# The last feature tile in two token halves, with the closing norm and the writes per half

## The chip, the cores and the metric

The kernel is one program on one core of a Trainium2 chip. The time is the device time of one execution, in microseconds. Before the change three runs gave 2014.44, 2014.51 and 2013.72, so the median is 2014.44. The profile is one further execution.

## The reference

Two blocks run one after the other on 512 tokens of 1024 features, in float32. The first is a transformer-like block. The second has two layers, each with a gated linear recurrence and a matrix memory beside each other. Only the end of the second block matters here:

```python
        y = jnp.concatenate([y_rg, y_ml], axis=-1) @ w_out[l]
        x = x + gate[:, None, :] * y
    return rms_norm(x, final_g)
```

So the last layer ends with a product by `w_out` (2048 by 1024), a gated addition to the residual, and a norm over all 1024 features of each token, scaled by `final_g`.

## The kernel before, in words

Activations lie transposed: features on the 128 partitions, the 512 tokens along the free axis. A tensor of 1024 features is eight tiles of 128x512, here called feature tiles, numbered `m`. Every float32 matrix product is three matmuls in a reduced format: `mm3` (L121 to L127) multiplies the high part of the weights by the high part of the activations (L125), high by low (L126) and low by high (L127).

Weights come as a stream of 512 KB chunks. For each chunk SyncE issues a DMA (L81), ScalarE rounds it to the high part (L96) and VectorE subtracts to get the low part (L98). By the time the last tile starts, all chunks have been loaded and split.

At the end of layer 1 the loop over `m` makes each feature tile of the output product from 16 input tiles `d`, so 48 matmuls of 512 columns into one bank of PSUM. VectorE multiplies the bank by the layer's gate and adds the residual (L1880; the tile is called `xr`). ScalarE squares the result (L149), and VectorE and GpSimd add the squares up (L153, L155, L159). `early` sums the first seven tiles' squares over the partitions, with matmuls against a column of ones (L165), in the middle of the last tile's products.

After the last tile the closing norm begins. `mean` sums the last tile's squares over the partitions (L165) and adds the early part (L180, tile `nms`). `rsqrt` is ten small VectorE operations (L207 to L214), each of which waits for the one ahead of it, and ends in `ncol`, one value for each token. `part2` spreads these values over all partitions with four matmuls against the identity (L195), and ScalarE copies the result to SBUF (L199, `nrow`). Then VectorE multiplies the eight feature tiles by `final_g` and `nrow` (L2041) and SyncE issues one write of 256 KB for each (L2042).

The program has no planner. Each engine takes its instructions strictly in the order in which the code issues them, and waits are on semaphores that count instructions of other engines.

Of the kernel before, what the change touches and what calls it, by code (L numbers as in the profile page):

```python
# [21 lines left out]
F32 = mybir.dt.float32  # L22
# [3 lines left out]
AF = mybir.ActivationFunctionType  # L26
OP = mybir.AluOpType
# [4 lines left out]
T = 512  # L32
DM = 1024
# [87 lines left out]
def mm3(k, ps, w, x, start, stop):  # L121


    mm = k.nc.tensor.matmul
    mm(ps, w[0], x[0], start=start, stop=False)  # L125
    mm(ps, w[0], x[1], start=False, stop=False)  # L126
    mm(ps, w[1], x[0], start=False, stop=stop)  # L127


class Norm:  # L130
# [9 lines left out]
    def add(self, src, scale=1.0):  # L140


        k, i = self.k, self.i
        own = i < 2 or (self.tail and i == self.n - 1)
        if own:
            sq = self.pool.tile([128, T], F32, name="nacc", bufs=3 if self.pool is k.work else 6)
        else:
            sq = k.work.tile([128, T], F32, name="nsq", bufs=2)
        k.nc.scalar.activation(sq, src, AF.Square, scale=scale)  # L149
        if own:  # L150
            self.acc.append(sq)
        elif i % 2:
            k.nc.gpsimd.tensor_add(self.acc[1], self.acc[1], sq)  # L153
        else:
            k.nc.vector.tensor_add(self.acc[0], self.acc[0], sq)  # L155
        self.i += 1
        if self.i == self.n - self.tail:
            eng = k.nc.vector if self.tail else k.nc.gpsimd
            eng.tensor_add(self.acc[0], self.acc[0], self.acc[1])  # L159
# [14 lines left out]
    def mean(self, eps=1e-6):  # L174
        k, v = self.k, self.k.nc.vector
        assert self.i == self.n
        self.ms = k.work.tile([128, 4], F32, name="nms", bufs=2)
        s = self.colsums(self.acc[2 if self.tail else 0])
        if self.tail:
            v.scalar_tensor_tensor(self.ms, s, 1.0 / DM, self.head, op0=OP.mult, op1=OP.add)  # L180
        else:
            v.tensor_scalar(self.ms, s, 1.0 / DM, eps, op0=OP.mult, op1=OP.add)
# [19 lines left out]
def rsqrt(k, out, ms):  # L202

    nc = k.nc
    shape = list(ms.shape)
    seed = k.work.tile(shape, I32, name="rseed", bufs=2)
    nc.vector.tensor_scalar(seed, ms.bitcast(I32), -0.5, 1597463007.0, op0=OP.mult, op1=OP.add)  # L207
    y = seed.bitcast(F32)
    for it in range(3):
        a = k.work.tile(shape, F32, name="rsa", bufs=2)  # L210
        nc.vector.tensor_mul(a, y, y)
        nc.vector.scalar_tensor_tensor(a, a, -0.5, ms, op0=OP.mult, op1=OP.mult)
        y2 = out if it == 2 else k.work.tile(shape, F32, name="rsy", bufs=2)
        nc.vector.scalar_tensor_tensor(y2, a, 1.5, y, op0=OP.add, op1=OP.mult)  # L214
        y = y2
# [11 lines left out]
def xtile(k, name, dtype=F32R):  # L227
    return k.xp.tile([128, T], dtype, name=name, tag="x", bufs=26)
# [29 lines left out]
def bank(k):  # L258
    k.nbank = (k.nbank + 1) % 2
    tag = ("pa", "pb")[k.nbank]  # L260
    return k.ps.tile([128, T], F32, name=tag + k.phase, tag=tag, bufs=2)
# [1109 lines left out]
def between(k, scr, nf, ng):  # L1371

    nc, v = k.nc, k.nc.vector
    gg = k.work.tile([128, 8], F32, name="gg")
    gf = k.vec[:, VEC["norm_final"][0]:VEC["norm_final"][0] + 8]
    v.tensor_mul(gg, gf, k.lay[0].gs)
    nf.part1(root=False)
    ng.mean()  # L1380
    ms = k.work.tile([128, 4], F32, name="nmt", bufs=2)
    v.scalar_tensor_tensor(ms, nf.ms, 1e-6, ng.ms, op0=OP.mult, op1=OP.add)
    ng.col = k.work.tile([128, 4], F32, name="ncol", bufs=2)
    rsqrt(k, ng.col, ms)
    k.tail[1]()
    ng.part2()
    k.tail[2]()
    xs = modulate(k, 0, ng, gg, scr)
    k.tail[3]()
    rsqrt(k, nf.col, nf.ms)  # L1390

    def root():
        nf.part2()

    def residual(d):
        v.scalar_tensor_tensor(k.h[d], k.h[d], gf[:, d:d + 1], nf.row, op0=OP.mult, op1=OP.mult)
        nc.sync.dma_start(scr["x"][d], k.h[d])
        k.dbg(f"x2{d}", k.h[d])
    return xs, [root] + [lambda d=d: residual(d) for d in range(8)]


def renorm(k, l, norm, scr):
    norm.part1()
    norm.part2()
    xs = modulate(k, l, norm, k.lay[l].gs, scr)
    return xs, [lambda d=d: k.nc.sync.dma_start(scr["x"][d], k.h[d]) for d in range(8)]
# [2 lines left out]
LAYER = """P24 U24 P25 U25 P20 qkv0 D P21 U20 U21 mi2 vw P22 U22 P23 U23 qkv1 D mi3 vw P0 U0 qkv2 vw D qkv3 g0 vw g1 P1 U1 ri0 P8 g2 D P9 U8 g3 hw0 hs0 U9 rg0 rq0 vr0 P26 U26 hn0 rs0 rs1 rz0 rz1 vr1 P27 U27 hw1 f0 P2 U2 hs1 D P3 U3 ri1 u F0 P32 U32 P33 U33 D rg1 rq1 hn1 rs2 P10 U10 P11 f1 rs3 U11 P29 U29 rz2 hw2 P28 rz3 vr2 U28 P4 U4 hs2 P5 U5 ri2 u P34 rg2 rq2 F1 U34 P35 U35 hn2 rs4 P12 D P13 f2 D U13 U12 rs5 P31 rz4 vr3 hw3 P30 rz5 U30 U31 P6 U6 P7 U7 ri3 D u hs3 D P36 F2 rg3 U36 P37 rq3 hn3 rs6 P14 U37 rs7 u P15 f3 U14 U15 rz6 P38 D F3 rz7 U38 D P39 U39 vw"""  # L1409


def layer(k, l, xs, aside, ins, scr, norm):


    nc, v = k.nc, k.nc.vector
    L = k.lay[l]
    with ExitStack() as st:
        pool = st.enter_context(k.tc.tile_pool(name=f"lay{l}", bufs=1))
# [323 lines left out]
        cat = {}  # L1742
# [120 lines left out]
        xr = {}  # L1863

        def x_read(m):
            if m < 8:
                xr[m] = xtile(k, "xr", F32)
                nc.sync.dma_start(xr[m], scr["x"][m])
        k.phase = f"out{l}"
        for m in range(8):  # L1870
            x_read(m)
        for m in range(8):
            ps = bank(k)
            for d in range(16):
                k.ws.hold = m == 7 and d >= 8
                if m == 7 and d == 10:
                    norm.early()
                mm3(k, ps, k.ws.get((f"w_out.{l}", d, m)), cat[d], d == 0, d == 15)
            k.h[m] = xr[m]
            v.scalar_tensor_tensor(k.h[m], ps, L.mod[:, 16 + m:17 + m], k.h[m], op0=OP.mult, op1=OP.add)  # L1880
            norm.add(k.h[m])
# [21 lines left out]
def body(tc, ins, out, dbg):  # L1903
    nc = tc.nc
    with ExitStack() as ctx:
        k = Ctx()
        k.nc, k.tc = nc, tc
        ctx.enter_context(tc.manual_schedule())
        pool = lambda name, bufs=1, **kw: ctx.enter_context(tc.tile_pool(name=name, bufs=bufs, **kw))
# [9 lines left out]
        scr = {"wq": dp.tile([2, 128, 128], F32, name="scr_wq"), "V": dp.tile([8, 128, 512], F32, name="scr_V"),  # L1919
               "C": dp.tile([8, 128, 512], F32, name="scr_C"), "T": dp.tile([8, 128, 512], F32, name="scr_T"),  # L1920
               "R": dp.tile([8, 2, 128, 256], F32, name="scr_R"), "u": dp.tile([512, 512], F32, name="scr_u"),
               "y": dp.tile([512, 512], F32, name="scr_y"), "x": dp.tile([8, 128, T], F32, name="scr_x"),
               "v": dp.tile([4, 2, 128, T], F32, name="scr_v")}
# [11 lines left out]
        for d in range(8):  # L1935
            t = xtile(k, "h", F32)
# [29 lines left out]
        norm = Norm(k, 8)  # L1966
        xs = []
# [31 lines left out]
        with tc.tile_pool(name="prep2", bufs=1) as pp:  # L1999
# [6 lines left out]
            with ple_p as lp:  # L2006
# [15 lines left out]
                with tc.tile_pool(name="sums", bufs=1) as np_:  # L2022
# [6 lines left out]
                    xs, aside = between(k, scr, nf, ng)  # L2029
        norm = None  # L2030
        for l in range(2):
            norm = Norm(k, 8, tail=True)
            k.phase = f"layer{l}"
            layer(k, l, xs, aside, ins, scr, norm)
            if l == 0:
                xs, aside = renorm(k, 1, norm, scr)
        norm.part1()
        norm.part2()
        for d in range(8):
            o = xtile(k, "out", F32)  # L2040
            nc.vector.scalar_tensor_tensor(o, k.h[d], k.v("final_g_2", d), norm.row, op0=OP.mult, op1=OP.mult)  # L2041
            nc.sync.dma_start(out[d * 128:(d + 1) * 128], o)  # L2042
        return k.ws


# [108 lines left out]
def build(dbg=None):  # L2154
    import concourse.bacc as _bacc
    import concourse.tile as _tile
    from concourse import mybir as _mybir
    nc = _bacc.Bacc("TRN2", target_bir_lowering=False, num_devices=1)
    ins = {n: nc.dram_tensor(f"in_{n}_dram", s, F32, kind="ExternalInput").ap() for n, s in SHAPES.items()}
    out = nc.dram_tensor("out_0_dram", (DM, T), F32, kind="ExternalOutput").ap()  # L2160
    d = {n: nc.dram_tensor(f"dbg_{n}_dram", s, F32, kind="ExternalOutput").ap() for n, s in (dbg or {}).items()}
    with _tile.TileContext(nc) as tc:
        ws = body(tc, ins, out, d)
    return nc, ws.order
# [8 lines left out]
```

## Time and profile before

| | us |
|---|---|
| median of the three runs | 2014.44 |
| profiled execution, device time | 2013.55 |
| its span, first to last instruction | 2011.8 |
| TensorE busy in the span | 1957.6 (97%) |
| VectorE busy | 1335.3 (66%) |
| ScalarE busy | 815.5 (41%) |
| GpSimd busy | 161.7 (8%) |
| last tile's first matmul starts | 1983.44 |
| last tile's last matmul starts | 1995.05 |
| closing products on VectorE start | 2003.40 |

The times of a trace run from the start of its span. A timeline row gives the start, the duration, the engine, the line and the operation, with what it writes left of the arrow and what it reads right of it. A duration with a count behind it covers that many instructions in a row. A bracket at the end is the idle time of the engine before, and what ended it.

### The profile page before, as it was taken

How to read it: one execution, taken by the hardware profiler on the slowest of the kernel's cores; microseconds unless marked ns; L12 is line 12 of the kernel's file. 1: busy time of each engine (PE TensorE's matmuls, PEld its weight loads, DVE VectorE, ACT ScalarE, POOL GpSimd, SP SyncE). 2: the span in 40 equal slices, each digit the busy share in tenths (PEclk: the TensorE clock that was granted, in tenths of full speed). 3: DMA queues.
4: the chain of work that ended last, by engine and by line, in shares of the span. 5: the costliest groups of instructions: out<-in, count | busy, mean ns of one | idle time of the engine just before them, and what ended most of it. 6: DMA issues, size and time to landing. Idle time of an engine off the chain costs nothing. (4 is left out here: it accounts for less than half of the span.)

```text
span 2011.8 us, 24981 instructions
## 1 busy us (share of the span) xinstructions
PE 1957.6 (97%) x9432; PEld 1603.7 (80%) x9432; DVE 1335.3 (66%) x2241; ACT 815.5 (41%) x1227; POOL 161.7 (8%) x219
## 2 busy tenths in 40 slices
PE   8999999997999999999999999999999899999997
PEld 6888888886767888888888787888888677888886
DVE  7766576678655577667666775877753765777733
ACT  5323233435554332323244355555532454455521
POOL 1000000210242100000001100110000100101000
PEclk9999999998999999999999799999999899999998
DMA  5334545455201455364532143222242142232241
GB/s 186 102 117 156 160 130 154 162 189 163 90 7 37 155 183 194 118 224 168 168 104 88 45 152 115 71 88 84 74 147 95 63 157 95 74 95 84 81 139 53
DMA packets 100377, 239.59 MB, mean 119 GB/s; under 512 B 24600, under 2 KB 35608, under 8 KB 100256
## 3 DMA queue, kind: packets, MB, share of 16 engines
q1 hardware_dynamic: 100112, 237.82, 36.4%
q8 instruction: 74, 1.21, 0.2%
q14 instruction: 47, 0.39, 0.1%
q10 hardware_dynamic: 144, 0.17, 0.0%
HBM read 215.67 MB, written 21.10 MB: 118 GB/s over the span
## 5 line engine op out<-in xcount | busy, mean ns | idle before, releaser
L98 DVE TENSOR_TENSOR wlo<-wstage,whi 128x1024 fp32r<-128x1024 f32 (+1 forms) x305 | 376.0, 1240 | 149.4 <-ACT whi L96 148.9
L96 ACT ACTIVATE whi<-wstage 128x1024 fp32r<-128x1024 f32 (+1 forms) x306 | 313.5, 1043 | 142.8 <-PE pasecond L126 36.1
L277 ACT ACTIVATE t<-t 128x512 f32<-128x512 f32 x44 | 27.8, 632 | 176.9 <-DVE t L276 176.9
L1223 DVE SCALAR_TENSOR_TENSOR adaa<-adaw,b2c,adaa 128x256 f32<-128x256 f32 x168 | 81.3, 484 | 5.1
L127 PE MATMUL pahead<-xnh,wlo 128*128 128x512 f32 x208 | 81.4, 391 | 2.8 <-DVE wlo L98 2.8
L125 PE MATMUL pahead<-xnh,whi 128*128 128x512 f32 x208 | 83.4, 401 | 0.0
L153 POOL TENSOR_TENSOR nacc<-nacc,nsq 128x512 f32<-128x512 f32 x20 | 26.8, 1342 | 682.0 <-ACT nsq L149 682.0
L126 PE MATMUL pahead<-xnl,whi 128*128 128x512 f32 x208 | 81.0, 390 | 0.0
L125 PE MATMUL pbhead<-xnh,whi 128*128 128x512 f32 x192 | 77.6, 404 | 0.0
L125 PE MATMUL pbfirst<-xnh,whi 128*128 128x512 f32 x176 | 70.4, 400 | 7.1 <-ACT whi L96 6.5
L126 PE MATMUL pbhead<-xnl,whi 128*128 128x512 f32 x192 | 76.0, 396 | 0.0
L127 PE MATMUL pbhead<-xnh,wlo 128*128 128x512 f32 x192 | 76.0, 396 | 0.0
L1454 DVE SCALAR_TENSOR_TENSOR conv<-cpad,vec,conv 128x512 f32<-128x512 f32 x96 | 72.2, 752 | 5.6
L126 PE MATMUL pbfirst<-xnl,whi 128*128 128x512 f32 x176 | 69.6, 395 | 0.3 <-DVE xnl L223 0.3
L127 PE MATMUL pbfirst<-xnh,wlo 128*128 128x512 f32 x176 | 69.1, 393 | 0.0
L125 PE MATMUL pasecond<-xnh,whi 128*128 128x512 f32 x176 | 69.0, 392 | 0.0
L125 PE MATMUL pbsecond<-xnh,whi 128*128 128x512 f32 x176 | 68.8, 391 | 0.0
L125 PE MATMUL pafirst<-xnh,whi 128*128 128x512 f32 x176 | 68.7, 390 | 0.0
L127 PE MATMUL pafirst<-xnh,wlo 128*128 128x512 f32 x176 | 68.6, 390 | 0.0
L127 PE MATMUL pasecond<-xnh,wlo 128*128 128x512 f32 x176 | 68.6, 390 | 0.0
L126 PE MATMUL pafirst<-xnl,whi 128*128 128x512 f32 x176 | 68.5, 389 | 0.0
L127 PE MATMUL pbsecond<-xnh,wlo 128*128 128x512 f32 x176 | 68.5, 389 | 0.0
(754 smaller groups left out, 5266.7 us busy)
## 6 DMA issues: line engine op xcount, KB each, us to landing
wstage<-in_wpack_dram SPq DMA_DIRECT2D x304, 512.0 KB, 3.7
adaw<-in_wada_dram SPq DMA_DIRECT2D x48, 512.0 KB, 4.8
scr_v<-vv SPq DMA_DIRECT2D x16, 256.0 KB, 2.1
vr<-scr_v SPq DMA_DIRECT2D x16, 256.0 KB, 4.4
xr<-scr_x SPq DMA_DIRECT2D x16, 256.0 KB, 5.9
h<-in_xT_dram SPq DMA_DIRECT2D x8, 256.0 KB, 5.8
s5vw<-scr_wq SPq DMA_DIRECT2D x64, 32.0 KB, 2.0
s5vb<-in_s5bq_dram SPq DMA_DIRECT2D x8, 256.0 KB, 2.7
```

Source lines behind the costliest of these rows:

```text
L96: k.nc.scalar.activation(hi[:, s], st[:, s], AF.Copy)
L98: eng.tensor_sub(lo[:, s], st[:, s], hi[:, s].bitcast(F32))
L125: mm(ps, w[0], x[0], start=start, stop=False)
L126: mm(ps, w[0], x[1], start=False, stop=False)
L127: mm(ps, w[1], x[0], start=False, stop=stop)
L153: k.nc.gpsimd.tensor_add(self.acc[1], self.acc[1], sq)
L277: nc.scalar.activation(t1, t1, AF.Silu)
L1223: v.scalar_tensor_tensor(a, w[:, d], cd, a, op0=OP.mult, op1=OP.add)
L1454: v.scalar_tensor_tensor(c, xp[:, 1 + j:1 + j + T], w(j), c, op0=OP.mult, op1=OP.add)
```

## The change

The eighth feature tile of the last layer is taken out of the loop and handed to a new function `ending`, which also takes the place of the closing norm. It works on two halves of 256 tokens:

- Four of the other feature tiles, `m` 2 to 5, are multiplied by `final_g` ahead of time, on ScalarE, into tiles called `hg`.
- The products of the eighth tile run twice over all 48 pairs of weights and activations, once for each half of the tokens, with 256 columns each. The order of the products is the same, and `early` stays at `d` = 10 of the first half.
- The partition sums, the inverse root and the spreading are done for each half. The sum over the first half sits between products of the second half (after `d` = 5). The spreading uses `transpose` in place of a product with the identity, and comes after all products.
- Of the closing products, GpSimd makes some from `hg` and the SBUF copy of the spread values, and VectorE makes the others from the residual tiles and the spread values where they lie in PSUM. In the first half VectorE makes tiles 0, 1, 6 and 7 and GpSimd tiles 2 to 5. In the second VectorE makes 0 to 3, 6 and 7 and GpSimd 4 and 5.
- Two feature tiles share one write of 256 KB, in pieces of 1 KB. Six are issued by SyncE, two by ScalarE.

```diff
+def ending(k, l, cat, h, norm, out):
...
+    for m in range(2, 6):
+        pre[m] = xtile(k, "hg", F32)
+        nc.scalar.activation(pre[m], h[m], AF.Copy, scale=g(m))
...
+    def products(half, at):
+        ps = bank(k)[:, :TH]
+        s = slice(half * TH, half * TH + TH)
+        for d in range(16):
+            if half == 0:
+                w[d] = k.ws.get((f"w_out.{l}", d, 7))
+            mm3(k, ps, w[d], (cat[d][0][:, s], cat[d][1][:, s]), d == 0, d == 15)
+            if d in at:
+                at[d]()
+        return ps
+
+    def add(half, ps):
+        s = slice(half * TH, half * TH + TH)
+        v.scalar_tensor_tensor(h[7][:, s], ps, gate, h[7][:, s], op0=OP.mult, op1=OP.add)
+        sq[half] = k.work.tile([128, T], F32, name="nsq", bufs=2)[:, :TH]
+        nc.scalar.activation(sq[half], h[7][:, s], AF.Square)
+
+    def mean(half):
+        ps = k.ps.tile([128, T], F32, name="pm", bufs=2)
+        for j in range(2):
+            nc.tensor.matmul(ps[:, j:j + 1], sq[half][:, j * 128:(j + 1) * 128], k.ones[:, :1], start=True, stop=True)
...
+        rsqrt(k, col[half], ms[half])
...
+    def wide(half):
+        pb = k.ps.tile([128, T], F32, name="pc", bufs=2)
+        for j in range(2):
+            nc.tensor.transpose(pb[:, j * 128:(j + 1) * 128], col[half][:, j:j + 1].to_broadcast([128, 128]), k.ident)
+        row = whole[:, half * TH:half * TH + TH]
+        nc.scalar.activation(row, pb[:, :TH], AF.Copy)
+        rows[half] = pb[:, :TH], row
+
+    def last(half, m, pool, queue):
...
+            if pool:
+                nc.gpsimd.tensor_mul(oi, pre[m + i][:, s], rows[half][1])
+            else:
+                v.scalar_tensor_tensor(oi, h[m + i][:, s], g(m + i), rows[half][0], op0=OP.mult, op1=OP.mult)
+        dst = out[m * 128:(m + 2) * 128, s].rearrange("(m p) t -> p m t", p=128)
+        queue.dma_start(dst, o.rearrange("p (m t) -> p m t", m=2))
+
+    ps = products(0, {10: norm.early})
+    add(0, ps)
+    ps = products(1, {5: lambda: mean(0)})
+    wide(0)
+    add(1, ps)
+    last(0, 2, True, nc.sync)
+    last(0, 4, True, nc.sync)
+    last(0, 0, False, nc.sync)
+    last(0, 6, False, nc.sync)
+    mean(1)
+    wide(1)
+    last(1, 4, True, nc.scalar)
+    last(1, 0, False, nc.sync)
+    last(1, 2, False, nc.scalar)
+    last(1, 6, False, nc.sync)
...
         for m in range(8):
+            if l and m == 7:
+                ending(k, l, cat, [k.h[i] for i in range(7)] + [xr[7]], norm, out)
+                break
...
-        norm.part1()
-        norm.part2()
-        for d in range(8):
-            o = xtile(k, "out", F32)
-            nc.vector.scalar_tensor_tensor(o, k.h[d], k.v("final_g_2", d), norm.row, op0=OP.mult, op1=OP.mult)
-            nc.sync.dma_start(out[d * 128:(d + 1) * 128], o)
```

VectorE at the end of the program, before the change. `xr` is the last residual tile, `nms` the mean square, `rseed`, `rsa`, `rsy` and `ncol` the inverse root, `out` a finished tile:

```order
L1880 SCALAR_TENSOR_TENSOR xr<-pbout_15951,mod_5931,xr 128x512 [waits PE_49]
L180 SCALAR_TENSOR_TENSOR nms<-pm,nhead 128x4 [waits DVE_49,PE_49]
L207 TENSOR_SCALAR rseed<-nms 128x4 [waits DVE_49]
L211 TENSOR_TENSOR rsa<-rseed 128x4 [waits DVE_49]
L212 SCALAR_TENSOR_TENSOR rsa<-rsa,nms 128x4 [waits DVE_49]
```

VectorE from the end of the first half's inverse root (`lcol`) to the start of the second half's (`lms`, `rseed`), after the change:

```order
L214 SCALAR_TENSOR_TENSOR lcol<-rsa,rsy 128x2 [waits DVE_49]
L1438 SCALAR_TENSOR_TENSOR xr<-paout_16019,mod_5931,xr 128x256 [waits PE_49]
L1471 SCALAR_TENSOR_TENSOR out<-xr,vec,pc 128x256 [waits Activation_49]
L1471 SCALAR_TENSOR_TENSOR out<-xr,vec,pc 128x256 x3
L1447 SCALAR_TENSOR_TENSOR lms<-pm,nhead 128x2 [waits PE_49]
L207 TENSOR_SCALAR rseed<-lms 128x2 [waits DVE_49]
L211 TENSOR_TENSOR rsa<-rseed 128x2 [waits DVE_49]
```

The first half's four products now stand between the second half's residual tile and its inverse root. Before, the inverse root came right behind the residual tile and the products came behind it.

ScalarE at the end, before (the squares `nsq` and `nacc`, the copy `nrow`):

```order
L96 ACTIVATE whi<-wstage 128x1024 [waits DMAHW0_49,PE_49,Activation_49]
L96 ACTIVATE whi<-wstage 128x1024 [waits DMAHW1_49,PE_49,Activation_49]
L149 ACTIVATE nsq<-xr 128x512 [waits DVE_49,Activation_49]
L149 ACTIVATE nacc<-xr 128x512 [waits DVE_49]
L199 ACTIVATE nrow<-pm 128x512 [waits PE_49]
```

and after, where `hg` are the four tiles multiplied ahead of time and the last two rows are writes:

```order
L149 ACTIVATE nsq<-xr 128x512 [waits DVE_49,Activation_49]
L1422 ACTIVATE hg<-xr,vec 128x512 x4
L1440 ACTIVATE nsq<-xr 128x256 [waits DVE_49,Pool_49]
L1459 ACTIVATE nrow<-pc 128x256 [waits PE_49]
L1440 ACTIVATE nsq<-xr 128x256 [waits DVE_49,Activation_49]
L1459 ACTIVATE nrow<-pc 128x256 [waits PE_49]
L1473 DMA out_dram<-out 128x2x256 [waits Pool_49]
L1473 DMA out_dram<-out 128x2x256 [waits DVE_49]
```

The second half's square now stands behind the copy of the first half's spread values.

TensorE at the end, after (`paout` is the second half's bank, `lcol` a half's inverse root, `pc` its spread values, `pm` the sums):

```order
L127 MATMUL paout_16019<-ymh,wlo 128x256
L1457 MATMUL pc<-ident,lcol 128x128 [waits DVE_49,PE_49]
L1457 MATMUL pc<-ident,lcol 128x128
L1445 MATMUL pm<-ones,nsq 128x1 [waits PE_49,Activation_49]
L1445 MATMUL pm<-ones,nsq 128x1
L1457 MATMUL pc<-ident,lcol 128x128 [waits DVE_49]
L1457 MATMUL pc<-ident,lcol 128x128
```

Where four sums and four products with the identity stood behind the last matmul, there are now two transposes of the first half, two sums and two transposes of the second.

## Rows read from the trace of the kernel before

**Rows 1.** the page's busy times: engine, us, share of the span, instructions

```profile
PE 1957.6 (97%) x9432; PEld 1603.7 (80%) x9432; DVE 1335.3 (66%) x2241; ACT 815.5 (41%) x1227; POOL 161.7 (8%) x219
```

**Rows 2.** the chain that ended last, from 1995 us: start us, us, what

```profile
1995.47 0.76 DVE xr L1880
1996.26 0.64 ACT nacc L149
1996.94 1.44 PE pm L165 x8
1998.41 0.17 DVE nms L180
2000.38 0.17 DVE ncol L214
2000.69 2.06 PE pm L195 x8
2002.78 0.61 ACT nrow L199
2004.82 3.98 DVE out L2041 x6
```

**Rows 3.** timeline of TensorE, last tile: start us, us, engine, line, operation

```profile
1983.44 0.39 PE L125 MATMUL pbout<-yrh,whi 128*128 128x512 f32 x1
1990.24 0.95 PE L165 MATMUL pm<-ones,nacc 128*128 128x1 f32 x8
1995.05 0.39 PE L127 MATMUL pbout<-ymh,wlo 128*128 128x512 f32 x1
```

**Rows 4.** timeline of VectorE, the sum of the first seven squares

```profile
1985.95 0.69 DVE L159 TENSOR_TENSOR nacc<-nacc 128x512 f32<-128x512 f32 x1
```

**Rows 5.** timeline of TensorE, first and last of 24 matmuls of 256 columns

```profile
1187.50 0.28 PE L1561 MATMUL pbgates<-whi,xmh 128*128 128x256 f32 x1
1190.26 0.28 PE L1563 MATMUL pagates<-whi,xml 128*128 128x256 f32 x1
```

**Rows 6.** timeline of TensorE's weight loads, the last of the same 24

```profile
1190.14 0.19 PEld L1563 LDWEIGHTS pagates<-whi,xml 128*128 128x128 f32 x1
```

**Rows 7.** windows: stretch, us, five engines busy, granted clock, DMA share, GB/s

```profile
149.60:150.20 0.60, 0.60 (x5) 0.48 (x4) 0.43 (x1) 0.60 (x2) 0.00 (x0) 1.00 1.01 340
2000.70:2002.80 2.10, 2.04 (x8) 1.74 (x8) 0.00 (x0) 0.03 (x1) 0.00 (x0) 0.50 0.00 0
2006.00:2006.50 0.50, 0.00 (x0) 0.00 (x0) 0.50 (x2) 0.00 (x0) 0.00 (x0) 0.50 1.03 397
```

**Rows 8.** timeline of ScalarE, the last square and the idle time before it

```profile
1996.26 0.63 ACT L149 ACTIVATE nacc<-xr 128x512 f32<-128x512 f32 x1 [11.14 <-DVE xr L1880]
```

**Rows 9.** timeline of TensorE, eight transposes of 128x128

```profile
554.98 1.04 PE L1023 MATMUL pc<-ident,csm 128*128 128x128 f32 x8
```

**Rows 10.** groups of ScalarE by form: xcount, busy us, mean ns, idle before

```profile
L858 ACT ACTIVATE cy<-pc 128x128 f32<-128x128 f32 x2 | 0.5, 267 | 1.5 <-PE pc L856 1.5
```

**Rows 11.** groups of VectorE by form, a product with a column of scalars

```profile
L1223 DVE SCALAR_TENSOR_TENSOR adaa<-adaw,b2c,adaa 128x256 f32<-128x256 f32 x168 | 81.3, 484 | 5.1
```

**Rows 12.** timeline of GpSimd, four products of 128x256

```profile
542.04 2.78 POOL L1007 TENSOR_TENSOR csm<-csm,cmask 128x256 f32<-128x256 f32 x4
```

**Rows 13.** timeline of VectorE, start of layer 1

```profile
1570.25 1.28 DVE L1352 TENSOR_TENSOR mt<-xr,pm 128x512 f32<-128x512 f32 x2 [2.86 <-ACT nrow L199]
1571.45 1.64 DVE L1360 TENSOR_SCALAR mx<-mt,gs,mod 128x512 f32<-128x512 f32 x1
1573.81 0.54 DVE L1360 TENSOR_SCALAR mx<-mt,gs,mod 128x512 f32<-128x512 f32 x1
```

**Rows 14.** timeline of GpSimd, start of layer 1

```profile
1570.30 2.52 POOL L1350 TENSOR_TENSOR mt<-xr,nrow 128x512 f32<-128x512 f32 x2 [27.45 <-ACT nrow L199]
```

**Rows 15.** timeline of VectorE, an inverse root while GpSimd works

```profile
1301.77 0.57 DVE L212 SCALAR_TENSOR_TENSOR rsa<-rsa,hms 128x4 f32<-128x4 f32 x1
```

**Rows 16.** timeline of GpSimd at the same time

```profile
1301.69 0.64 POOL L1654 TENSOR_SCALAR_AFFINE_SELECT Wd<-Wd 128x512 f32<-128x512 f32 x1 [12.32 <-ACT Wd L1653]
```

More of the change, by code (lines that the diff above doesn't have):

```diff
@@ L1409 @@
 LAYER = """P24 U24 P25 U25 P20 qkv0 D P21 U20 U21 mi2 vw P22 U22 P23 U23 qkv1 D mi3 vw P0 U0 qkv2 vw D qkv3 g0 vw g1 P1 U1 ri0 P8 g2 D P9 U8 g3 hw0 hs0 U9 rg0 rq0 vr0 P26 U26 hn0 rs0 rs1 rz0 rz1 vr1 P27 U27 hw1 f0 P2 U2 hs1 D P3 U3 ri1 u F0 P32 U32 P33 U33 D rg1 rq1 hn1 rs2 P10 U10 P11 f1 rs3 U11 P29 U29 rz2 hw2 P28 rz3 vr2 U28 P4 U4 hs2 P5 U5 ri2 u P34 rg2 rq2 F1 U34 P35 U35 hn2 rs4 P12 D P13 f2 D U13 U12 rs5 P31 rz4 vr3 hw3 P30 rz5 U30 U31 P6 U6 P7 U7 ri3 D u hs3 D P36 F2 rg3 U36 P37 rq3 hn3 rs6 P14 U37 rs7 u P15 f3 U14 U15 rz6 P38 D F3 rz7 U38 D P39 U39 vw"""
-def layer(k, l, xs, aside, ins, scr, norm):
+def ending(k, l, cat, h, norm, out):
+    nc, v = k.nc, k.nc.vector
+    gate = k.lay[l].mod[:, 23:24]
+    TH = T // 2
+    g = lambda m: k.v("final_g_2", m)
+    pre = {}
+    for m in range(2, 6):
+        pre[m] = xtile(k, "hg", F32)
+        nc.scalar.activation(pre[m], h[m], AF.Copy, scale=g(m))
+    w, sq, ms, col = {}, {}, {}, {}
+    def products(half, at):
[17 more added lines that the diff above has]
+            nc.tensor.matmul(ps[:, j:j + 1], sq[half][:, j * 128:(j + 1) * 128], k.ones[:, :1], start=True, stop=True)
+        ms[half] = k.work.tile([128, 2], F32, name="lms", bufs=2)
+        v.scalar_tensor_tensor(ms[half], ps[:, :2], 1.0 / DM, norm.head[:, 2 * half:2 * half + 2], op0=OP.mult, op1=OP.add)
+        col[half] = k.work.tile([128, 2], F32, name="lcol", bufs=2)
+        rsqrt(k, col[half], ms[half])
+    rows = {}
+    whole = k.work.tile([128, T], F32, name="nrow", bufs=1)
+    def wide(half):
[6 more added lines that the diff above has]
+    def last(half, m, pool, queue):
+        s = slice(half * TH, half * TH + TH)
+        o = xtile(k, "out", F32)
+        for i in range(2):
+            oi = o[:, i * TH:i * TH + TH]
+            if pool:
[19 more added lines that the diff above has]
+    last(1, 6, False, nc.sync)
@@ L1415, in layer @@
+def layer(k, l, xs, aside, ins, scr, norm, out):
     nc, v = k.nc, k.nc.vector
@@ L2033, in body @@
             k.phase = f"layer{l}"
-            layer(k, l, xs, aside, ins, scr, norm)
+            layer(k, l, xs, aside, ins, scr, norm, out)
             if l == 0:
                 xs, aside = renorm(k, 1, norm, scr)
-        norm.part1()
-        norm.part2()
-        for d in range(8):
-            o = xtile(k, "out", F32)
-            nc.vector.scalar_tensor_tensor(o, k.h[d], k.v("final_g_2", d), norm.row, op0=OP.mult, op1=OP.mult)
-            nc.sync.dma_start(out[d * 128:(d + 1) * 128], o)
         return k.ws
```

## Prediction

> **What bounds the kernel now.** I read the page's busy times first: TensorE is busy for 97% of the span [rows 1], so elsewhere only TensorE's work counts. Then the chain that ended last, from 1995 us on, since the change lies there [rows 2]. In it the reader is to see a string of steps with one engine working at a time: residual tile 0.76, square 0.64, partition sums 1.44, the inverse root from 1998.41 to 2000.55, spreading 2.06, copy 0.61, and eight closing products from 2003.40 (0.02 behind the copy) to 2008.80. The span ends 3.0 us later, at 2011.8, with the last write. From the last matmul's result at 1995.45 that is 16.4 us, all that the change can shorten. The DMA engines are full during the closing products: share 1.03 at 397 GB/s [rows 7], so a 256 KB write takes 0.66 us and the eight take 5.28, as long as the products.
>
> **The products in halves (loss).** The last tile starts at 1983.44, its sums stand 30 matmuls later at 1990.24, its last matmul at 1995.05 [rows 3]. That is 6.80/30 = 0.227 us a matmul, and 0.96 for the four early sums (11.61 less 47 x 0.227). The early sums need the sum of seven squares, ready at 1986.64 [rows 4]; the new stream gets there at 1983.44 + 30 x 0.12 = 1987.04, so they still don't wait, by 0.4 us. For 256 columns, 24 matmuls of layer 0 start between 1187.50 and 1190.26, 2.76/23 = 0.120 us apart [rows 5]. So 96 x 0.120 = 11.52 stand for 48 x 0.227 = 10.88. The first half's own sums, two in place of four, add about half of 0.96, 0.48. The second half's last matmul starts at 1983.44 + 95 x 0.12 + 0.96 + 0.48 = 1996.28 and its result is there 0.28 later, at 1996.56: **1.1 us later than before**.
>
> A load of weights lasts 0.19 us [rows 6], longer than the 0.12 between two matmuls, and the row is from the stream of rows 5; so loads overlap there, and I count none. [...]
>
> **What is hidden.** The four tiles multiplied ahead are four ScalarE instructions like the 0.63 us square, 2.5 us in the 11.14 that ScalarE is idle [rows 8]; uncovered they would cost 2.5. The first half's sums and inverse root lie beside the second half's products: the root takes the 2.14 of rows 2 and is done by about 1995.3, 1.1 before TensorE wants it.
>
> **Between the last matmul and the second inverse root.** Two transposes: eight take 1.04 [rows 9], 0.27 for the first and 0.11 for each further, so 0.38, from 1996.40 to 1996.78. The copy of 256 columns isn't in the trace. It lies between 0.27 for 128 columns [rows 10] and 0.61 for 512 [rows 2]; on the line between them 0.38. Copy: 1996.80 to 1997.18. The residual half on VectorE takes 0.48, by a product of the same size and kind [rows 11], to 1997.06; but its square is queued behind the copy on ScalarE and so goes from 1997.20 to 1997.61 (0.64 less 256 columns of that line, 0.41). Two sums take 0.7 to 0.8, half of 1.44: ready at 1998.4.
>
> VectorE is not. Ahead of the second root it has the first half's four products, which wait for the copy. Eight products of 512 columns start 0.66 apart [rows 2] where one lasts 0.75; for 256 columns that is 0.48 and 0.40 for each further: 1.68, from 1997.20 to 1998.88. Then the mean, to 1999.1.
>
> **GpSimd beside the root (the term I am least sure of).** GpSimd makes four products from 1997.20; four of this size take 2.78 [rows 12], so to 1999.98. At the start of layer 1 VectorE's products with one operand in PSUM run at 0.64 each beside GpSimd, but its next operation, on SBUF alone, takes 1.64 where the same takes 0.54 later [rows 13], and ends 0.3 after GpSimd's pair [rows 14]: it was held over both. A root's operation of 128x4 took 0.57 in place of 0.16 and ended with a GpSimd instruction that had started 0.08 before it [rows 15, 16]. The root's steps read SBUF alone, so I hold them until 1999.98. The bounds are 0 (as if GpSimd weren't there) and 0.9; I take the full 0.9, since both pairs of rows show a hold to the end. Ten steps of 0.196 then end at 1999.98 + 1.96 = 2001.94.
>
> **To the end.** TensorE has then idled over 3 us. [...] I take 0.75, as nothing has worked since the sums: with 0.14 to start, as before the spreading, done at 2002.83. Copy 0.40 to 2003.23. VectorE makes six products, 0.48 + 5 x 0.40 = 2.48, to 2005.73; GpSimd's two (1.4) and ScalarE's issues end within that. By the old tail of 3.0 the end is 2008.74.
>
> But the writes bound it too. Before, the first product was done at 2004.15, 5.28 of transfer followed, and the end came at 2011.8: 2.37 besides the transfer. Now the first pair is done at 2003.25 + 0.88 = 2004.13 and four writes follow: 2004.13 + 2.37 + 2.64 = 2009.14, later than 2008.74. The first half's four writes are out by then. Pieces of 1 KB are new here. A stretch in which the rotation tables, also in 1 KB pieces, are written shows 340 GB/s [rows 7], which would make the four writes 3.08; the other bound is no change. Halfway adds 0.2: **2009.35**.
>
> Sum: 2011.8 to 2009.35 is a gain of 2.4 us, out of a 1.1 loss in the products, 0.9 of holding, and shorter steps. The profiled execution took 2013.55, its span and 1.75 around it; the median is 0.89 above that. I take the gain off the median: 2014.44 - 2.4 = **2012.0**. That is 0.12%, under the 0.2% (4.0 us) that a measurement of this kernel can tell from no change.
>
> **Rivals.** *No hold.* VectorE's small steps slip between GpSimd's products. Root from 1998.88, done 2001.04, everything after it 0.9 earlier: 2011.1, and 2010.7 if TensorE also keeps the upper clock level for the last transposes. [...] Against: rows 13 to 16. Only with a further half us from somewhere is it faster by more than 0.2%.
>
> *Full exclusion.* The closing products on VectorE also read a scalar column from SBUF, which those of rows 13 did not; if that makes them wait for GpSimd too, the two engines work in turn. First-half products on VectorE from 1999.98 to 2001.66, root to 2003.82, spreading 2004.71, copy 2005.11, GpSimd's pair 1.4, VectorE's six 2.48, to 2009.0, and the end at 2012.0 plus 0.2 for small pieces: 2014.8, no gain. For it: the scalar; against: that it is one value per partition.
>
> *Weight loads set the pace.* The halved stream comes at 0.19 a matmul, the length of a load [rows 6], in place of 0.12. That is 96 x 0.07 = 6.7 more: 2018.7, slower. It decides from 0.145 a matmul on, where the gain of 2.4 is used up. Against it: rows 5, with loads of the same size and type. For it: that stream is only 24 long.
>
> *Half-rate writes.* 1 KB pieces move at half the rate: 2.64 more at the end, 2014.6. The 340 GB/s of rows 7 speak against it.
>
> **How the numbers follow.** Forecast 0.53, with its own range of 2011.2 to 2012.8. No hold 0.23, of which 0.12 goes past 4.0 us with help I can't name. Full exclusion 0.14, half-rate writes 0.05, load-bound 0.05. The range reaches from below the best no-hold case (2010.7 less 0.5, somewhat over half the 0.8 by which the three runs differ) to full exclusion: 2010.2 to 2014.9. Faster by over 0.2% is 0.12, slower by over 0.2% is the load-bound case, 0.05, and the rest, 0.83, is within.
>
> **What would show it.** In the new profile: matmuls of the last tile 0.12 apart and its last result 1.1 us later than 1995.45; the second square starting right behind the copy of the first half; `lms` of the second half starting behind VectorE's fourth product and not behind its sums; one of the root's first steps stretched to the end of GpSimd's fourth product; the granted clock 0.50 at the last transposes; and the DMA engines without a gap over the last four writes. The forecast is wrong if the matmuls come at 0.15 or more, if VectorE's four products take over 2.5 us beside GpSimd's, or if the second root takes its plain 2.1 us while GpSimd works.

## The result, and the profile after

Four runs of the changed kernel took 2041.38 to 2045.13 us, median 2043.36; the kernel before took 2014.43 beside it. The ratio is 1.0144, with a 95% interval of 1.0127 to 1.0162. So the change made the kernel 29 us slower, where 2.4 us of gain were forecast, and the time lies far outside the range.

The profiled execution took 2044.05 us with a span of 2042.3. First its page's busy times, to be held against [rows 1]:

```profile
PE 1992.1 (98%) x9476; PEld 1606.4 (79%) x9476; DVE 1337.2 (65%) x2255; ACT 818.2 (40%) x1233; POOL 166.2 (8%) x225
```

TensorE is busy 34.5 us longer. The other engines are within 5 us of before, and the clock in the profile's 40 slices is no lower (mean granted clock 0.982, before 0.980). Next the place: the last tile's first matmul started at 1983.44 before [rows 3]; after it starts at 2016.75 (below). So 33.3 us had been lost before the first instruction that the change rewrote. From that matmul to the span's end it was 2011.8 - 1983.44 = 28.36 us, and is 2042.3 - 2016.75 = 25.55 now. The rewritten tail does gain, 2.8 us.

The loss shows once TensorE's instructions are grouped by line and form (tile names, shapes, count, busy us, mean ns of one, idle before). Three groups of 512-column matmuls that the change doesn't touch, before:

```profile
L125 PE MATMUL pafirst<-xnh,whi 128*128 128x512 f32 x176 | 68.7, 390 | 0.0
L127 PE MATMUL pbsecond<-gh,wlo 128*128 128x512 f32 x88 | 34.3, 389 | 0.0
L125 PE MATMUL paout<-yrh,whi 128*128 128x512 f32 x64 | 24.9, 389 | 0.0
```

and after:

```profile
L125 PE MATMUL pafirst<-xnh,whi 128*128 128x512 f32 x176 | 69.7, 396 | 0.0
L127 PE MATMUL pbsecond<-gh,wlo 128*128 128x512 f32 x88 | 34.7, 395 | 0.0
L125 PE MATMUL paout<-yrh,whi 128*128 128x512 f32 x64 | 25.3, 395 | 0.0
```

Each lasts about 6 ns longer, in every stage of the program and with no new idle time before it. The starts say the same. TensorE's timeline of the kernel before, nine matmuls of one product, first and last:

```profile
1953.75 0.39 PE L126 MATMUL paout<-yrl,whi 128*128 128x512 f32 x1
...
1955.56 0.39 PE L125 MATMUL paout<-yrh,whi 128*128 128x512 f32 x1
```

and seven after:

```profile
1983.86 0.39 PE L125 MATMUL paout<-yrh,whi 128*128 128x512 f32 x1
...
1985.26 0.39 PE L125 MATMUL paout<-yrh,whi 128*128 128x512 f32 x1
```

That is 1.81/8 = 0.226 us from start to start before and 1.40/6 = 0.233 after. Over the 6864 matmuls of `mm3` that still have 512 columns, the mean of one goes from 393.2 to 398.3 ns; 6864 x 5.1 ns = 35 us, about the 33.3 us that were lost ahead of the last tile.

The tail, from the timeline of all engines after (start us, us, engine, line, operation, tiles, count):

```profile
2016.75 0.28 PE L125 MATMUL pbout<-yrh,whi 128*128 128x256 f32 x1
...
2020.55 0.28 PE L127 MATMUL pbout<-ymh,wlo 128*128 128x256 f32 x1
...
2029.70 0.48 DVE L1438 SCALAR_TENSOR_TENSOR xr<-paout,mod,xr 128x256 f32<-128x256 f32 x1 [1.55 <-PE paout L127]
2029.91 0.38 ACT L1459 ACTIVATE nrow<-pc 128x256 f32<-128x256 f32 x1 [5.36 <-PE pc L1457]
2030.27 0.42 ACT L1440 ACTIVATE nsq<-xr 128x256 f32<-128x256 f32 x1
2030.33 1.66 DVE L1471 SCALAR_TENSOR_TENSOR out<-xr,vec,pc 128x256 f32<-128x256 f32 x4
2030.37 2.77 POOL L1469 TENSOR_TENSOR out<-hg,nrow 128x256 f32<-128x256 f32 x4 [21.77 <-ACT nrow L1459]
2030.74 0.61 PE L1445 MATMUL pm<-ones,nsq 128*128 128x1 f32 x4 [0.87 <-ACT nsq L1440]
...
2031.90 0.15 DVE L1447 SCALAR_TENSOR_TENSOR lms<-pm,nhead 128x2 f32<-128x2 f32 x1
2032.09 0.40 DVE L207 TENSOR_SCALAR rseed<-lms 128x2 int32<-128x2 int32 x1
2032.52 0.64 DVE L211 TENSOR_TENSOR rsa<-rseed 128x2 f32<-128x2 f32 x1
2033.19 0.16 DVE L212 SCALAR_TENSOR_TENSOR rsa<-rsa,lms 128x2 f32<-128x2 f32 x1
...
2034.78 0.69 PE L1457 MATMUL pc<-ident,lcol 128*128 128x128 f32 x2 [3.43 <-DVE lcol L214]
2035.51 0.38 ACT L1459 ACTIVATE nrow<-pc 128x256 f32<-128x256 f32 x1 [4.81 <-PE pc L1457]
2035.92 2.44 DVE L1471 SCALAR_TENSOR_TENSOR out<-xr,vec,pc 128x256 f32<-128x256 f32 x6 [1.20 <-ACT nrow L1459]
```

The chain of [rows 2] is here in two overlapping halves. Of the root's small steps two are long, 0.40 and 0.64, and each ends with a product of GpSimd: the first at 2032.49 with the third (2030.37 + 3 x 0.69 = 2032.44), the second at 2033.16 with the fourth (2030.37 + 2.77 = 2033.14). And the windows of the last spreading and of the last writes (columns as in [rows 7]):

```profile
2034.70:2035.50 0.80, 0.69 (x2) 0.29 (x2) 0.02 (x1) 0.00 (x0) 0.00 (x0) 0.50 1.03 343
...
2038.00:2039.00 1.00, 0.00 (x0) 0.00 (x0) 0.36 (x1) 0.00 (x0) 0.00 (x0) 0.50 1.04 339
```

**Where the difference can come from.** No instruction ahead of the last tile differs in kind, shape or order. What does differ is the place of the tiles in SBUF. The compiled program gives every tile a byte address in its partition, one pool behind the other. `lms` and `lcol` are new tiles of the pool `work`; with two buffers of each and the rounding of sizes they make the pool longer, and the pools behind it start 128 bytes later. The next one, `xp`, begins at byte 78464 instead of 78336, which is 306 x 256. With it move the right-hand operands of `mm3` (`xnh`, `gh`, `ymh`, `yrh` and their low parts), called moving operands below: they lay on multiples of 512 bytes and now lie 128 behind one. The split weights (`whi`, `wlo`) lie ahead of `work`, on multiples of 512 in both kernels.

### The profile page after: what moved, and what is told of

It is laid out like the page before. It is cut to its first block, busy times and chain, and to the rows that moved or that the text cites. A ratio compares the mean times of both kernels' runs of the same rounds, so it can differ in the third digit from the quotient of the medians.

```text
span 2042.3 us, 25098 instructions
## 1 busy us (share of the span) xinstructions
PE 1992.1 (98%) x9476; PEld 1606.4 (79%) x9476; DVE 1337.2 (65%) x2255; ACT 818.2 (40%) x1233; POOL 166.2 (8%) x225
## 5 line engine op out<-in xcount | busy, mean ns | idle before, releaser
L126 PE MATMUL pasecond<-xnl,whi 128*128 128x512 f32 x176 | 69.4, 395 | 0.0
```

## Experiments

### Is it the place of the tiles?

Three runs, each compared with the kernel before on the same chip. The first gives the changed kernel the old addresses:

```diff
-        ms[half] = k.work.tile([128, 2], F32, name="lms", bufs=2)
+        ms[half] = k.work.tile([128, 4], F32, name="nms", bufs=2)[:, :2]
-        col[half] = k.work.tile([128, 2], F32, name="lcol", bufs=2)
+        col[half] = k.work.tile([128, 4], F32, name="ncol", bufs=2)[:, :2]
```

> The changed kernel, with the two small work tiles it adds (lms and lcol, two columns each) taken as slices of the tiles nms and ncol that were there before; no instruction is added or left out, and every later pool starts where it did in the kernel before. Theory (place in SBUF): the 33 us that were lost ahead of the last tile come from the 128 bytes by which the new tiles moved every later pool, so they go: the 512-column fp32r matmuls start 0.2267 us apart again, the last tile begins at about 1983.4 us of the span, and the time is 2014.4 - 2.8 = 2011.6 us (2010.8 to 2012.6). Rival (code): it is the other program text or the order of the code that makes each matmul longer; then the pitch stays at 0.2334 us and the time at about 2043 us.

Measured: 2011.94 us against 2014.68, ratio 0.9986 (0.9977 to 0.9994). The group is back at its old mean:

```profile
L125 PE MATMUL paout<-yrh,whi 128*128 128x512 f32 x64 | 24.9, 389 | 0.0
```

The whole loss went with the two tiles, 2043.36 - 2011.94 = 31.4 us by the medians, and the kernel is 2.7 us below the one before. The last tile began at 1984.83 rather than 1983.4: executions differ by some us ahead of it, so the tails below are counted from the last tile's first matmul. This one takes 2010.2 - 1984.83 = 25.4 us.

The second shifts the kernel before:

```diff
+        k.work.tile([128, 32], F32, name="gap", bufs=1)
```

> The kernel before, instruction for instruction, with one unused tile of 128 bytes a partition in the pool work, so that every later pool starts 128 bytes further on, as in the changed kernel. Theory (place in SBUF): the 512-column matmuls go from 0.2267 to 0.2334 us, and the time to 2014.4 + 33.3 = 2047.7 us (2044 to 2050). Rival (code): no instruction differs, so 2014.4 us within 0.2%.

Measured: 2045.7 us, ratio 1.0148 (1.0135 to 1.0162), and

```profile
L125 PE MATMUL paout<-yrh,whi 128*128 128x512 f32 x64 | 25.2, 394 | 0.0
```

An unused tile alone makes all of the loss, so neither the new code nor the tail has a part in it.

The third leaves the changed kernel its tiles and fills up to 512 bytes:

```diff
+                k.work.tile([128, 96], F32, name="gap", bufs=1)
```

> The changed kernel with its two new tiles and an unused one of 384 bytes beside them, so that every later pool starts 512 bytes further on than in the kernel before. Theory (it is the remainder of the address by 512 that counts): pitch 0.2267 us, 2011.6 us as in the run with the old addresses. Rival (any other address than the old one, or less room at the end of SBUF): 2043 us. Rival (code): 2043 us.

Measured: 2013.02 us, ratio 0.9987 (0.9978 to 0.9997). Other addresses than before, but the same remainder, and no loss.

### Which address, and how far

The next moves one pair of operands only, those of the first feed-forward product:

```diff
-GAPS = {"base": 288, "ffn1": 320, "ffn2": 0, "lay": 320, "mix2": 224, "ple": 192}
+GAPS = {"base": 288, "ffn1": 448, "ffn2": 0, "lay": 320, "mix2": 224, "ple": 192}
```

> The kernel before with the gap ahead of one pool (that of the first feed-forward product) made 128 bytes larger, so that only that pool's gh and gl, the moving operands of 528 matmuls, lie 128 bytes behind a multiple of 512; all other tiles stay. Theory (each matmul pays for the place of its own moving operand): only the groups that read this pool's gh and gl go from 389 to 395 ns in the mean of one, and the time rises by 528 x 0.0065 = 3.4 us to 2017.9 us. Rival (a property of the program as a whole, such as its layout or its code): all groups change or none, 2014.4 or about 2047 us.

Measured: 2017.53 against 2014.68, ratio 1.0015 (1.0006 to 1.0024), and in the groups, moved ones first:

```profile
L127 PE MATMUL pafirst<-gh,wlo 128*128 128x512 f32 x88 | 34.8, 395 | 0.0
L126 PE MATMUL pafirst<-gl,whi 128*128 128x512 f32 x88 | 34.7, 395 | 0.0
...
L127 PE MATMUL pbsecond<-gh,wlo 128*128 128x512 f32 x88 | 34.3, 389 | 0.0
L126 PE MATMUL pbsecond<-gl,whi 128*128 128x512 f32 x88 | 34.3, 389 | 0.0
```

Each matmul pays for the place of its own operand, 6 ns; 528 of them make 3.2 us, and 2.9 was measured.

Now other distances, in the kernel before, by an unused tile of 256, 64 and 192 bytes in place of the 128. Each is a single execution, so a difference under some 4 us says nothing there.

> The kernel before with an unused tile of 256 bytes in the pool work: all moving operands of the 512-column matmuls lie 256 bytes behind a multiple of 512. If a multiple of 256 is enough, 389 ns in the mean of one matmul and 2014.7 us; if only a multiple of 512 is free of cost, 395 ns and about 2046 us as at 128; if the cost goes with the distance, something between or beyond, up to twice the 31 us.

Measured: 2014.80 us, so 256 bytes are as good as 0.

```profile
L125 PE MATMUL paout<-yrh,whi 128*128 128x512 f32 x64 | 24.9, 389 | 0.0
```

> The kernel before with an unused tile of 64 bytes in the pool work: all moving operands 64 bytes behind a multiple of 512. If any remainder costs the same, 395 ns and about 2046 us; if the cost goes with the distance, half of it, about 2030 us; if 64 bytes are still free, 389 ns and 2014.7 us.

Measured: 2027.52 us, and the three kinds of matmul fall apart, not in the same way in every product. The last product of a layer first (`out`), then one of the first block (`mixout`):

```profile
L125 PE MATMUL paout<-yrh,whi 128*128 128x512 f32 x64 | 25.2, 394 | 0.0
...
L127 PE MATMUL paout<-yrh,wlo 128*128 128x512 f32 x64 | 25.1, 392 | 0.0
L126 PE MATMUL paout<-yrl,whi 128*128 128x512 f32 x64 | 24.8, 388 | 0.0
...
L127 PE MATMUL pbmixout<-oh,wlo 128*128 128x512 f32 x16 | 6.3, 394 | 0.0
...
L125 PE MATMUL pbmixout<-oh,whi 128*128 128x512 f32 x16 | 6.2, 388 | 0.0
```

In `out` high by high pays 5 ns, low weights by high 3, high weights by the low part nothing. In `mixout` low weights by high pays the 5, high weights by the low part 3 (392), and high by high nothing. So the same three prices change places, and being high or low doesn't decide which one a matmul pays. Their mean, 2.3 ns, would make 16 us over the 6912 such matmuls of the kernel before; 12.8 were measured. That the sum came out near half was the middle guess; that the kinds differ was not foreseen.

> The kernel before with an unused tile of 192 bytes in the pool work: moving operands 192 bytes behind a multiple of 256, the weights on one. If what counts is how far the distance is from a multiple of 256, to either side, as at 64 bytes: 2027.5 us, with 394, 388 and 392 ns for L125, L126 and L127. If it grows with the remainder up to 256: 395 ns or more and 2046 us or more.

Measured: 2048.99 us, with the three kinds near 396 in this product:

```profile
L125 PE MATMUL paout<-yrh,whi 128*128 128x512 f32 x64 | 25.3, 396 | 0.0
```

By time alone 192 bytes can't be told from 128; by the mean over all 512-column matmuls of `mm3`, 398.9 ns against 397.9, they cost a little more. The cost is not the same to both sides of a multiple of 256: 64 on one side costs 13 us, 64 on the other 34.

Last, the weights. The gap ahead of their pool is made 128 bytes larger; in one run, a single execution, the moving operands are filled up to the next multiple of 512, in the other they shift along.

```diff
-GAPS = {"base": 288, "ffn1": 320, "ffn2": 0, "lay": 320, "mix2": 224, "ple": 192}
+GAPS = {"base": 416, "ffn1": 320, "ffn2": 0, "lay": 320, "mix2": 224, "ple": 192}
...
+        k.work.tile([128, 96], F32, name="gap", bufs=1)
```

> The kernel before with the gap ahead of the pool of weights 128 bytes larger and 384 unused bytes in the pool work: the split weights (whi, wlo) lie 128 bytes behind a multiple of 512, and the moving operands, 512 bytes further on, on multiples of 512. Theory (the moving operand's address counts, not the weights'): 389 ns and 2014.7 us. Rival (the distance between weights and moving operand, or the weights' own address): 395 ns and about 2046 us.

Measured: 2045.16 us and 394 ns:

```profile
L125 PE MATMUL paout<-yrh,whi 128*128 128x512 f32 x64 | 25.2, 394 | 0.0
```

My theory fell here. The moving operands lie where they cost nothing before, and yet all of the loss is back. The run without the filling tells the two rivals apart:

> The kernel before with only the gap ahead of the pool of weights 128 bytes larger: the split weights (whi, wlo) and the moving operands of the 512-column matmuls both lie 128 bytes behind a multiple of 256. Theory A (the distance between the weights and the moving operand, by the remainder of 256, is what counts, so the two reads get in each other's way): 389 ns in the mean of one matmul and 2014.7 us. Theory B (each operand's own address counts): at least as slow as with one of them moved, 395 ns and 2045 us, or up to 401 ns and 2076 us if the two add.

Measured: 2015.55 against 2015.48, ratio 0.9995 (0.9986 to 1.0005), and

```profile
L125 PE MATMUL paout<-yrh,whi 128*128 128x512 f32 x64 | 24.9, 389 | 0.0
```

With both off by 128 nothing is lost. What counts in these runs is the distance between the weights and the moving operand, by its remainder of 256: 0 is free, 64 costs about 13 us, 128 about 31, 192 about 34. The timelines show loads of weights beside running matmuls, 0.19 us each [rows 6]; that the two reads get in each other's way, as theory A has it, no run shows. Why the three kinds differ at 64, and what decides which of them pays, stays open, and no other remainder was run.

### The tail

The run with the old addresses shows what still stands in the tail. VectorE's timeline there, behind the second half's sum:

```profile
1998.50 1.66 DVE L1471 SCALAR_TENSOR_TENSOR out<-xr,vec,pc 128x256 f32<-128x256 f32 x4
...
2000.07 0.15 DVE L1447 SCALAR_TENSOR_TENSOR nms<-pm,nhead 128x2 f32<-128x2 f32 x1
2000.26 0.40 DVE L207 TENSOR_SCALAR rseed<-nms 128x2 int32<-128x2 int32 x1
2000.69 0.64 DVE L211 TENSOR_TENSOR rsa<-rseed 128x2 f32<-128x2 f32 x1
```

To test the hold, half of the first half's products go behind the second root. This run and the next also have the old addresses; the small copy on GpSimd is there to make its second pair wait for the root:

```diff
     last(0, 2, True, nc.sync)
-    last(0, 4, True, nc.sync)
     last(0, 0, False, nc.sync)
-    last(0, 6, False, nc.sync)
     mean(1)
+    nc.gpsimd.tensor_copy(k.work.tile([128, 4], F32, name="nms", bufs=2)[:, :2], col[1])
+    last(0, 4, True, nc.sync)
     wide(1)
+    last(0, 6, False, nc.sync)
```

> The changed kernel with the old addresses, and of the first half's eight products only four ahead of the second inverse root: GpSimd makes one pair (m = 2, 3) and VectorE one (0, 1); GpSimd's second pair (4, 5) waits for the second root's column by a small copy of it, and VectorE's second pair (6, 7) comes behind that root, while TensorE spreads it. Theory (VectorE's tensor-tensor steps are held while GpSimd works): in the run with the old addresses the means waited until 2000.07 for VectorE's four products, though the sums were done at about 1999.6, and the two steps after them took 0.40 and 0.64 instead of 0.16 to 0.17 us; with GpSimd done at about 1.4 us after its start, both are 0.16 to 0.17, the second root's column is ready 1.2 us earlier, and the time is 2011.9 - 1.2 = 2010.7 us (0.25% under the kernel before's 2014.7 becomes 0.2% or more; 2010.0 to 2011.5). Rival (no hold: those two steps are long for another reason, such as the first use of the tile): only the 0.5 us of the wait for VectorE goes, 2011.4 us. Rival (the writes are the bound): the column is earlier, the span is not, 2011.9 us.

Measured: 2012.17 us against 2014.74, ratio 0.9991 (0.9982 to 1.0). VectorE:

```profile
1999.82 0.16 DVE L1447 SCALAR_TENSOR_TENSOR nms<-pm,nhead 128x2 f32<-128x2 f32 x1 [0.18 <-PE pm L1445]
2000.02 0.23 DVE L207 TENSOR_SCALAR rseed<-nms 128x2 int32<-128x2 int32 x1
2000.28 0.16 DVE L211 TENSOR_TENSOR rsa<-rseed 128x2 f32<-128x2 f32 x1
```

and the windows of the end:

```profile
2004.00:2005.00 1.00, 0.00 (x0) 0.00 (x0) 1.00 (x4) 0.00 (x0) 0.99 (x2) 0.50 0.46 161
2005.00:2006.00 1.00, 0.00 (x0) 0.00 (x0) 0.64 (x2) 0.00 (x0) 0.00 (x0) 0.50 1.09 381
2006.00:2007.00 1.00, 0.00 (x0) 0.00 (x0) 0.00 (x0) 0.00 (x0) 0.00 (x0) 0.50 1.09 384
2007.00:2008.00 1.00, 0.00 (x0) 0.00 (x0) 0.00 (x0) 0.00 (x0) 0.00 (x0) 0.50 1.09 385
2008.00:2009.00 1.00, 0.00 (x0) 0.00 (x0) 0.00 (x0) 0.00 (x0) 0.00 (x0) 0.50 0.75 262
```

The hold is real: with GpSimd done at 2000.22 (its two products start at 1998.81 and take 1.41), the step of 0.64 takes 0.16, and the one of 0.40 takes 0.23 and ends at 2000.25. Counted from the second half's sum, the last copy comes 1.15 us earlier than in the run with the old addresses (2002.79 - 1998.13 = 4.66, against 2003.68 - 1997.87 = 5.81). But the tail takes 25.1 us instead of 25.4: of the 1.15 us that the column gained 0.3 are left, so the rival was right that the writes are the bound. What moves from 2004 to 2009, at 161, 381, 384, 385 and 262 GB/s in the five us, is 1.57 MB, so six writes: the two that were put behind the root and the last four. The DMA engines are full from 2005 to 2008, at a share of 1.09, and the last write that SyncE issues takes 3.6 us to land, where it took 2.6 with the old addresses.

The last run therefore gets the first half's row early instead, so that its writes go out early as well:

```diff
+    def first():
+        wide(0)
+        last(0, 2, True, nc.sync)
+        last(0, 0, False, nc.sync)
+
-    ps = products(1, {5: lambda: mean(0)})
-    wide(0)
+    ps = products(1, {5: lambda: mean(0), 12: first})
     add(1, ps)
-    last(0, 2, True, nc.sync)
     last(0, 4, True, nc.sync)
-    last(0, 0, False, nc.sync)
     last(0, 6, False, nc.sync)
```

> The changed kernel with the old addresses, and the first half's row of inverse roots made while the second half's products still run: its spread comes after the 13th of 16 block rows, then one pair of products on GpSimd (m = 2, 3) and one on VectorE (0, 1) ahead of the second half's sum, the other two pairs behind it as before. All four writes of the first half are still issued before the second root is done, unlike in the run that put two of them behind it. Counted from the last tile's first matmul: the second half's sum at 13.35 us instead of 13.04 (the spread now stands ahead of the last three block rows), the means at 15.0, held until GpSimd's fourth product ends at 15.6, the second column at 17.6 instead of 18.1, the end at 24.9 instead of 25.4 us (before: 28.4). Theory (hold, and writes of the first half out of the way): 24.9 us, about 2011.5 us in all, which the times alone can't tell from 2011.9. Rival (writes bound the end anyway): 25.1 us or more. Rival (the wait of TensorE for the first column costs more than the 0.3 us): the second half's sum later than 13.6 us, the end at 25.4 us or more.

Measured: 2011.61 us against 2015.48, ratio 0.9980 (0.9971 to 0.9988). The last tile begins at 1988.63 here, and the timeline goes on:

```profile
2001.26 2.79 POOL L1469 TENSOR_TENSOR out<-hg,nrow 128x256 f32<-128x256 f32 x4 [20.46 <-ACT nrow L1459]
2002.01 0.48 DVE L1438 SCALAR_TENSOR_TENSOR xr<-paout,mod,xr 128x256 f32<-128x256 f32 x1
...
2003.69 0.16 DVE L1447 SCALAR_TENSOR_TENSOR nms<-pm,nhead 128x2 f32<-128x2 f32 x1 [0.43 <-PE pm L1445]
...
2004.11 0.16 DVE L211 TENSOR_TENSOR rsa<-rseed 128x2 f32<-128x2 f32 x1
...
2005.89 0.43 PE L1457 MATMUL pc<-ident,ncol 128*128 128x128 f32 x2 [2.24 <-DVE ncol L214]
```

and the windows:

```profile
2005.00:2006.00 1.00, 0.11 (x1) 0.11 (x2) 0.69 (x5) 0.00 (x0) 0.00 (x0) 1.00 1.10 383
2006.00:2007.00 1.00, 0.32 (x2) 0.08 (x2) 0.22 (x1) 0.38 (x1) 0.18 (x1) 0.87 0.45 156
2007.00:2008.00 1.00, 0.00 (x0) 0.00 (x0) 1.00 (x4) 0.00 (x0) 1.00 (x2) 0.50 0.00 0
```

The sum comes at 2002.01 - 1988.63 = 13.38 us (expected 13.35), and the span ends at 2012.9 - 1988.63 = 24.3, better than the 24.9 expected. GpSimd ended at 2004.05, just ahead of the step that it would have held, and the last spreading started at a granted clock of 1.00, where it was 0.50 in the changed kernel, and took 0.43 instead of 0.69. The first half's writes are out before the second half's come: from 2007 to 2008 the DMA share is 0.00. This version beats both kernels, the one before by 0.2%; of 28.4 us of tail it saves 4.1, and the medians differ by 3.9.

## Why the prediction was wrong

**The step that failed** is the sum: "I take the gain off the median". It carries everything ahead of the last tile over from before as it was, without a reason given, and calls the 16.4 us behind the last matmul "all that the change can shorten". That the two tiles `lms` and `lcol` take room, and that every later tile moves with them, was never priced: a term put at nothing. The move alone is worth +31 us (the shifted kernel before, against 2014.68), over ten times what the tail gained. None of the rivals had it: the load-bound case looked for a slower TensorE in the halved stream only. A hint stood in the code: the table of gaps puts unused tiles of 192 to 320 bytes between pools, which serve nothing but the addresses.

**The tail**, point by point, by the trace after:

- *Products in halves, 0.12 apart.* Right. 32 steps from 2016.75 to 2020.55 make 0.119, and `xr` starts 12.95 us after the first matmul, where it was 12.03 [rows 2, 3]: 0.9 later, forecast 1.1. The two sets of sums between the products cost 0.8 and 0.4, where 0.96 and 0.48 were counted. The first set comes behind 33 products, not 30: it is now issued behind those of `d` = 10, and before it was issued ahead of them; it still waits for nothing. The trace shows a load of weights of 0.19 us beside each product, so the loads overlap here as in the stream of [rows 5, 6], and the load-bound case is refuted.
- *The second square behind the copy, copy 0.38, four products 1.68, the mean behind the fourth.* Right: 0.38 and 1.66; the square starts at 2030.27 as the copy ends, and the mean at 2031.90, though the sums end at 2031.35.
- *GpSimd holds the root to its fourth product's end.* Right in place, slightly too dear: the root and its mean take 2.82 us (2031.90 to 2034.72), against 2.14 in the last run, where nothing holds them for more than 0.02: 0.7, forecast 0.9. The prediction put all ten steps behind the fourth product; two of them were done by its end, one with the third product and one with the fourth. No hold and full exclusion are both refuted.
- *Transposes at the lower clock, 0.75.* 0.69, at a granted clock of 0.50. The 0.75 was my estimate, and no run shows it; in the last run, which starts them at 1.00, they took 0.43.
- *Writes bound the end.* Right. They move at 339 to 343 GB/s, the slow bound, of which I had taken half. That bound was right by luck. It was taken for a price of small pieces, but with the old addresses the same 1 KB pieces move at 381 and 383 GB/s (the windows of the last two runs). What the slow rows share is the place: in the compiled programs the rotation tables of the 340 GB/s row [rows 7] lie 192 bytes behind a multiple of 256, and the changed kernel's `out` tiles 128. Last product to the span's end is 2042.3 - 2038.36 = 3.9 us, forecast 3.6. Half-rate writes are refuted.

Together the tail gained 2.8 us against 2.4 forecast; the run with the old addresses is 2.7 below the kernel before (1.2 to 4.6).

## What to carry to other kernels

A new tile of a few bytes moves every tile that is allocated after it, so compare the addresses of the two compiled programs as well as their instructions; reusing tiles that are there moved nothing here. In a kernel bound by TensorE, look whether the mean of one untouched matmul changed before you look for waits: a few ns in each of 7000 is tens of us. When a tail is cut in halves, a wait that is removed only pays as far as the writes behind it are not queued behind others: 1.15 us of an earlier column gave 0.3 us here.

## What the hardware showed that was not expected

- A 512-column matmul whose moving operand lies 64, 128 or 192 bytes (modulo 256) further than its weights takes up to 5, 6 or 7 ns more than the 389; with both shifted by 128, nothing. At 64 the price of one is 5, 3 or 0 ns, and which kind pays which differs from product to product. The 256-column matmuls of the tail don't pay: 0.119 us apart at 128, 0.120 at 0 (1984.83 to 1988.66 for 32, in the run with the old addresses).
- The last writes also depend on where the tile lies that they read, here by its own address. Pieces of 2 KB moved at 391 to 402 GB/s from multiples of 256 bytes (the kernel before, with 256 bytes of shift, and with the weights alone moved, where the matmuls are slow) and at 375 to 389 from 64, 128 or 192 behind one, both moved by 128 included; pieces of 1 KB at 380 to 387 (the tail's runs with the old addresses) and at 339 to 343 (the changed kernel). Why the place of a tile changes the rate of its write, no run shows.
